# Rows of running decay sums through DRAM instead of through broadcast matmuls

## The chip, the cores and the metric

The kernel runs on one core of a Trainium2 chip. The metric is the device time of one execution in microseconds; the median over repeated executions stands for a kernel. Profiles come from one further execution that the hardware profiler records.

## The reference

Two layers of a decoder trunk work on 512 tokens of width 1024, all in float32. Each layer has a mixer and a gated feed-forward block with norms around both. The mixer projects the normed input into two groups: eight heads of dilated sliding-window attention, and four heads of a gated delta rule over chunks of 64 tokens. What the change touches is a part of the delta rule:

```python
g = jnp.cumsum(g, axis=-1)                       # within a chunk of 64 tokens
decay = jnp.exp(jnp.where(tril, g[..., :, None] - g[..., None, :], -jnp.inf))
kb = k * beta[..., None]
A = jnp.where(strict, jnp.einsum('bhnik,bhnjk->bhnij', kb, k) * decay, 0.0)
T = lax.linalg.triangular_solve(A + eye, eye, left_side=True, lower=True, unit_diagonal=True)
...
qk = jnp.einsum('bhnik,bhnjk->bhnij', q, k) * decay
```

For each head and each chunk a matrix of decays is needed: the exponential of the difference of two running sums, one that varies along the row and one along the column.

## The kernel before, in words

**Engines and helpers.** Every engine call goes through one helper (line 54), which gives the call a priority. So every row of a profile says L54, and the tiles' names tell where a row belongs. A scheduler then orders each engine's instructions by those priorities. Work that runs side by side is written as generators, which `nc.weave` interleaves: each has a number of steps and a stretch of the stage over which the steps are spread. Line numbers below are those of this kernel.

**The stage around the change.** In each layer, the channels of the delta rule's keys are projected first (`chan_proj` with `key`), woven with `decay()`, which makes the small vectors of the delta rule: `gr` holds the log decays, 128 tokens by 16 (four token blocks t times four heads h), and a matmul with the triangular matrix `tri` gives the running sums, whose negative is `ng`. Then five streams are woven: `dense` (32 steps: the q, k and v projections of the attention with four weight pieces each, four blocks of the delta rule's values, four of its queries, and the gate), `prepare` (16 steps over the first 0.43 of the stage), `attention` (from 0.52 to 0.9), `invert` (from 0.66 to 0.83) and `scan` (from 0.82 to 0.96).

**prepare().** After transposing the keys, it goes through the four token blocks. For each it makes the decay matrices `G` of the four heads: four matmuls broadcast a column of `gr` against `tri` into PSUM, VectorE adds `ng` (one value a partition) and the mask `dmask`, and ScalarE takes the exponential. Then PE multiplies the keys with themselves (`kT`), VectorE scales the product by `bb` and `G` into `U`, SP's queue stores `U` in the DRAM tile `dU`, and PE transposes `U` into `UT`. When all four `U` are stored, four loads, one a head, bring the diagonal 32 x 32 blocks back as `Lb` (64 KB each). GpSimd solves these blocks by forward substitution, 31 steps of a product (`Xt`) and a subtraction (`X`), and stores the result in `dX` by its own queue.

**invert().** For each token block GpSimd loads the solved blocks (`zc`) and clears `Z`, VectorE transposes the blocks into `Z`, and PE builds the whole inverse from them and `UT`; its first matmuls are `pw<-Z,UT`.

**Weights.** A weight piece (512 KB) is loaded by SP into one of three buffers `st`; ScalarE rounds it to `wh` (three buffers), VectorE, or for two pieces a layer GpSimd, takes the rest into `wl`, and PE uses both. The pieces of the attention are named `in_w_at`, those of the delta rule's channels `in_w_dn`. A buffer `st` is free for the next load when `wl` is done. SP carries all loads and stores named here in one order, except those of `dX` and `zc`.

**Buffers.** `G`, `UT`, `Kt`, `Z` and others share 41 buffers of one pool (`big`). The products in PSUM (`pw`) share four.

## Time and profile before

| | us |
|---|---|
| median of three runs | 1352.19 (1351.63 to 1352.3) |
| the profiled execution | 1352.82 |
| its span, first to last instruction | 1350.6 |
| PE busy | 1309.6 |
| VectorE busy | 1011.2 |
| ScalarE busy | 728.6 |
| GpSimd busy | 193.1 |

The profiled execution has 2.2 us outside its span. Its mean granted TensorE clock is 0.993 of full speed. A row of a timeline gives the start, the duration, the engine, the line, the operation with its output and inputs, the shape, how many instructions it stands for, and in brackets how long the engine had been idle and what ended that. PE is TensorE, DVE is VectorE, ACT is ScalarE, POOL is GpSimd; SPq and POOLq are the queues from which SyncE and GpSimd issue transfers.

### The profile page before, as it was taken

Reading aid. Unit: us, or ns where it says so; the run is one execution under the profiler, and the core shown is the slowest. Engines: PE = TensorE matmul, PEld = TensorE weight load, DVE = VectorE, ACT = ScalarE, POOL = GpSimd, SP = SyncE. Lnnn points to the kernel's source line nnn. Section 1 sums busy time; section 2 is a strip of 40 time slices with the busy share of each in tenths; the row PEclk is TensorE's granted clock in tenths of the full one; section 3 lists DMA queues with packets and bytes.
Section 4 is the critical chain, followed back from the end, with each engine's and each line's share of the span. In section 5 each row is a group of like instructions: output and inputs, shape, how many; then the busy total and the mean of one; then the engine's idle time right before and its main releaser. Section 6 shows DMA issues by size and latency. Waiting matters only on the chain.

```text
span 1350.6 us, 19526 instructions
## 1 busy us (share of the span) xinstructions
PE 1309.6 (97%) x6952; PEld 1090.6 (81%) x6952; DVE 1011.2 (75%) x1966; ACT 728.6 (54%) x1488; POOL 193.1 (14%) x250
## 2 busy tenths in 40 slices
PE   7999999999999999999999999998999999999997
PEld 6888877877988888887788877777888888888875
DVE  6565988868577787798777668888667767888885
ACT  5534976565333444467556369566543334444772
POOL 1007521011000000030010293102010000001201
PEclk8999999999999999999999999999999999999999
DMA  6233221244476566365651322104345666653664
GB/s 213 60 105 79 83 67 36 70 134 140 140 221 229 189 218 206 110 182 179 211 173 40 112 92 73 51 19 132 118 126 185 190 230 190 226 180 116 190 190 150
DMA packets 74274, 191.04 MB, mean 141 GB/s; under 512 B 13249, under 2 KB 13761, under 8 KB 74178
## 3 DMA queue, kind: packets, MB, share of 16 engines
q1 hardware_dynamic: 73666, 188.76, 44.4%
q0 software_dynamic: 512, 1.05, 0.4%
q8 instruction: 55, 0.90, 0.3%
q14 instruction: 41, 0.34, 0.1%
HBM read 159.89 MB, written 29.88 MB: 141 GB/s over the span
## 4 chain that ended last, share of the span: by engine, by line
PE 81%; DVE 8%; ACT 6%; DMA 2%; POOL 2%; issue 2%; SPq 0%; POOLq 0%; DVEq 0%; ACTq 0%
PE pm L54 68%; PE pw L54 12%; DVE wl L54 2%; ACT junk L54 2%; DVE xs L54 1%; ACT wh L54 1%; DMA st<-in_w_f 1%; POOL nr L54 1%; DVE x L54 1%; DVE xf L54 1%; ACT sc L54 1%; DMA stb<-in_w_ba 0%; POOL qs L54 0%; DVE KL L54 0%; POOL wl L54 0%
## 5 line engine op out<-in xcount | busy, mean ns | idle before, releaser
L54 DVE TENSOR_TENSOR wl<-st,wh 128x1024 fp32r<-128x1024 f32 (+1 forms) x246 | 280.9, 1146 | 164.7 <-ACT wh L54 163.6
L54 PE MATMUL pm<-hh,wh 128*128 128x512 f32 (+1 forms) x1024 | 374.4, 367 | 5.2 <-ACT hh L54 4.4
L54 PE MATMUL pm<-hl,wh 128*128 128x512 f32 (+1 forms) x1024 | 376.1, 368 | 2.2 <-DVE hl L54 2.2
L54 PE MATMUL pm<-hh,wl 128*128 128x512 f32 (+1 forms) x1024 | 374.9, 366 | 0.0
L54 ACT ACTIVATE wh<-st 128x1024 fp32r<-128x1024 f32 (+1 forms) x254 | 245.3, 971 | 239.2 <-PE pm L54 213.3
L54 PEld LDWEIGHTS pm<-hh,wh 128*128 128x128 f32 x1024 | 195.0, 191 | 35.5 <-ACT hh L54 4.8
L54 PEld LDWEIGHTS pm<-hl,wh 128*128 128x128 f32 x1024 | 195.9, 191 | 31.6 <-DVE hl L54 2.4
L54 PEld LDWEIGHTS pm<-hh,wl 128*128 128x128 f32 x1024 | 195.9, 191 | 29.3
L54 PE MATMUL pm<-wh,xf 128*128 128x512 f32 x528 | 164.5, 390 | 0.4 <-ACT wh L54 0.4
L54 PE MATMUL pm<-wh,hh 128*128 128x512 f32 x384 | 154.2, 404 | 0.0
L54 PE MATMUL pm<-wh,hl 128*128 128x512 f32 x384 | 152.7, 398 | 0.0
L54 PE MATMUL pm<-wl,hh 128*128 128x512 f32 x384 | 150.6, 394 | 0.8 <-DVE wl L54 0.8
L54 DVE SCALAR_TENSOR_TENSOR fgu<-pm,fw,fgu 128x511 f32<-128x511 f32 (+1 forms) x176 | 131.2, 746 | 23.1 <-ACT fgu L54 21.1
L54 PEld LDWEIGHTS pm<-wh,xf 128*128 128x128 f32 x528 | 99.0, 188 | 21.9 <-ACT wh L54 0.8
L54 PE MATMUL pm<-wl,xf 128*128 128x512 f32 x264 | 103.6, 392 | 0.8 <-DVE wl L54 0.8
L54 POOL TENSOR_TENSOR g<-g 128x256 f32<-128x256 f32 x22 | 25.4, 1173 | 494.2 <-DVE xf L54 494.2
L54 PEld LDWEIGHTS pm<-wl,hh 128*128 128x128 f32 x384 | 72.3, 188 | 15.0 <-DVE wl L54 1.8
L54 PEld LDWEIGHTS pm<-wh,hl 128*128 128x128 f32 x384 | 72.3, 188 | 14.1
L54 PEld LDWEIGHTS pm<-wh,hh 128*128 128x128 f32 x384 | 72.0, 188 | 14.2 <-ACT wh L54 0.5
L54 ACT ACTIVATE sc<-sc,mx 128x128 f32<-128x128 f32 (+3 forms) x128 | 69.5, 558 | 22.1 <-DVE mx L54 21.6
L54 ACT ACTIVATE fgu<-pm,fb,fw 128x512 f32<-128x512 f32 x88 | 66.9, 760 | 19.8 <-PE pm L54 19.8
L54 ACT ACTIVATE fgu<-fgu 128x512 f32<-128x512 f32 x44 | 27.8, 632 | 90.8 <-DVE fgu L54 90.8
(226 smaller groups left out, 1831.4 us busy)
## 6 DMA issues: line engine op xcount, KB each, us to landing
st<-in_w_f SPq DMA_DIRECT2D x118, 512.0 KB, 3.7
ws<-in_w_f SPq DMA_DIRECT2D x88, 256.0 KB, 4.6
T<-ws SPq DMA_DIRECT2D x66, 256.0 KB, 2.3
st<-in_w_at SPq DMA_DIRECT2D x32, 512.0 KB, 3.7
st<-T SPq DMA_DIRECT2D x30, 512.0 KB, 3.6
st<-in_w_dn SPq DMA_DIRECT2D x24, 512.0 KB, 3.7
st<-in_w_out SPq DMA_DIRECT2D x16, 512.0 KB, 3.7
U<-ws SPq DMA_DIRECT2D x22, 256.0 KB, 2.2
```

What stands on the lines that cost most here:

```text
L54: r = f(*args, **kwargs)
```

## The change

In each layer the 16 broadcast matmuls are gone. One matmul `gr`ᵀ · `tri` gives the same running sums with the 16 (block, head) pairs on partitions and the tokens along the row; VectorE copies them to `gt`, and SP stores them as `dG`, 16 x 128 values in DRAM. For each token block one load on SP then reads that block's four rows, 2 KB, to all 128 partitions of `G`. VectorE's additions work in place on `G` instead of reading PSUM. All else in `prepare` stands as it was.

```diff
         Gs, UT, Z = [], [], []
+
+        dG = dp.tile([NT * H, P], F32, name="dG")
 ...
             nc.scalar.activation(egl, pg[:, 16:], AF.Exp)
+
+            pgt = ps4(shape=(P, P))
+            nc.tensor.matmul(pgt[:16], gr, tri, start=True, stop=True)
+            gt = sp.tile([16, P], F32, name="gt", bufs=1)
+            nc.vector.tensor_copy(gt, pgt[:16])
+            nc.sync.dma_start(dG, gt)
             nc.vector.tensor_tensor(bd, pg[:, 16:], ng, op=OP.add)
 ...
             for t in range(NT):
-                pg2 = ps4()
+                G = big("G", shape=(P, H, P))
+                nc.sync.dma_start(G.rearrange("p h i -> p (h i)"), bcast(dG, H * P, t * H * P))
                 for h in range(H):
                     i = t * H + h
-                    nc.tensor.matmul(pg2[:, h, :], gr[:, i:i + 1].to_broadcast([P, P]), tri, start=True, stop=True)
-                G = big("G", shape=(P, H, P))
-                for h in range(H):
-                    i = t * H + h
-                    nc.vector.scalar_tensor_tensor(G[:, h, :], pg2[:, h, :], ng[:, i:i + 1], dmask,
+                    nc.vector.scalar_tensor_tensor(G[:, h, :], G[:, h, :], ng[:, i:i + 1], dmask,
                                                    op0=OP.add, op1=OP.add)
```

The scheduler orders the instructions anew. On SP, from the store of the first `U` to the last load of `Lb`, the first layer had this order before (the number behind a name is that of the buffer; the first `st` rows here are loads of v's pieces, the last is the first of `in_w_dn`):

```order
L54 DMA dU_588<-U_838 128x512
L54 DMA st_1234<-in_w_at 128x1024
L54 DMA st_1297<-in_w_at 128x1024
L54 DMA dU_588<-U_894 128x512
L54 DMA st_1340<-in_w_at 128x1024
L54 DMA dU_588<-U_966 128x512
L54 DMA dU_588<-U_995 128x512
L54 DMA Lb_823<-dU_588 16x32x32
L54 DMA st_1346<-in_w_at 128x1024
L54 DMA Lb_823<-dU_588 16x32x32 x3
```

With the change it has this one, from the store of the third `U` on; `st_1532` to `st_1864` are the first four pieces of `in_w_dn`:

```order
L54 DMA dU_594<-U_960 128x512
L54 DMA G_977<-dG_225 128x512
L54 DMA st_1532<-in_w_dn 128x1024
L54 DMA st_1657<-in_w_dn 128x1024
L54 DMA dU_594<-U_985 128x512
L54 DMA Lb_829<-dU_594 16x32x32 x2
L54 DMA st_1758<-in_w_dn 128x1024
L54 DMA Lb_829<-dU_594 16x32x32
L54 DMA st_1864<-in_w_dn 128x1024
L54 DMA Lb_829<-dU_594 16x32x32
```

The stores of `U` and the loads of `Lb` have moved back among the weight loads: the last `Lb` stood ahead of the first piece of `in_w_dn`, and now stands behind the fourth. Each of the second to fourth loads of `G` stands just behind the store of the `U` before it.

On VectorE, the rows around the fourth `U` before, where `wl_1067` belongs to k's last weight piece and `wl_1237` to v's first:

```order
L54 TENSOR_TENSOR wl_1067<-st_1064,wh_1066 128x1024
L54 SCALAR_TENSOR_TENSOR G_959<-pw_954,ng_217,dmask_88 128x128 x4
L54 SCALAR_TENSOR_TENSOR U_966<-pw_965,bb_215,G_959 128x128 x4
L54 SCALAR_TENSOR_TENSOR G_988<-pw_983,ng_217,dmask_88 128x128 x4
L54 SCALAR_TENSOR_TENSOR U_995<-pw_994,bb_215,G_988 128x128 x4
L54 TENSOR_TENSOR wl_1237<-st_1234,wh_1236 128x1024
```

And with the change, where `wl_1290` and `wl_1333` belong to v's second and third piece:

```order
L54 TENSOR_TENSOR r1_1154<-pm_920,rope_94 128x512
L54 TENSOR_TENSOR wl_1290<-st_1287,wh_1289 128x1024
L54 SCALAR_TENSOR_TENSOR G_977<-G_977,ng_217,dmask_88 128x128
L54 TENSOR_TENSOR wl_1333<-st_1330,wh_1332 128x1024
L54 SCALAR_TENSOR_TENSOR G_977<-G_977,ng_217,dmask_88 128x128 x3
L54 SCALAR_TENSOR_TENSOR U_985<-pw_984,bb_215,G_977 128x128 x4
L54 TENSOR_TENSOR r2_1155<-pm_920,rope_94 128x8x32 x2
```

The fourth `U` stood ahead of the split of v's first piece and now stands behind that of v's third.

On PE, the rows with the change around the first transpose of the first `U` (`U_840`); the keys' products for the second `U` (`kT`) are among them:

```order
L54 MATMUL pw_850<-ident_80,U_840 128x128
L54 MATMUL pw_857<-ident_80,r1_794 128x128
L54 MATMUL pw_850<-ident_80,U_840 128x128
L54 MATMUL pw_891<-kT_418 128x128
L54 MATMUL pw_850<-ident_80,U_840 128x128
L54 MATMUL pw_891<-kT_485 128x128
L54 MATMUL pw_850<-ident_80,U_840 128x128
L54 MATMUL pw_891<-kT_517 128x128
L54 MATMUL pw_891<-kT_586 128x128
L54 MATMUL pw_857<-ident_80,r1_794 128x128 x3
```

Behind them stand 20 matmuls of 128x512 for k, and then the first transpose of the second `U`. The broadcast matmuls that stood among such rows are gone; the matmuls of the dense work keep their order. On PE from the first `pw<-Z,UT` on, and on GpSimd throughout, the order is the one of before.

## The prediction

> **What bounds the kernel now.** I read the page's busy times first, then its chain of waits, then the group of the removed matmuls.

> ```profile
> PE 1309.6 (97%) x6952; PEld 1090.6 (81%) x6952; DVE 1011.2 (75%) x1966; ACT 728.6 (54%) x1488; POOL 193.1 (14%) x250
> PE 81%; DVE 8%; ACT 6%; DMA 2%; POOL 2%; issue 2%; SPq 0%; POOLq 0%; DVEq 0%; ACTq 0%
> ```

> TensorE is busy 97% of the span and carries 81% of the chain; GpSimd is busy 14%. So a matmul taken out counts, unless PE then meets something that was on time only because PE was no earlier. In each layer one such thing exists: the substitution X on GpSimd, whose result PE needs as `Z`. The timelines of GpSimd, VectorE and PE show how it ends (columns: start, us, engine, line, operation, count, idle time before it and what ended it):

> ```profile
> 105.72 0.23 POOL L54 TENSOR_TENSOR Xt<-Lb,X 64x31 f32<-64x31 f32 x1 [33.66 <-DMA Lb<-dU]
> 152.37 2.71 POOL L54 DMA_DIRECT2D dX<-X  x4 [0.31 <-POOL X L54]
> 166.88 2.40 POOL L54 TENSOR_TENSOR wl<-st,wh 128x1024 fp32r<-128x1024 f32 x1 [11.80 <-ACT wh L54]
> 174.55 0.59 POOL L54 DMA_DIRECT2D zc<-dX  x1 [5.26 <-DVE pTh L54]
> 175.15 2.42 POOL L54 TENSOR_TENSOR wl<-st,wh 128x1024 fp32r<-128x1024 f32 x1
> 177.51 0.53 POOL L54 MEMSET Z<- 128x512 f32 x1
> 178.07 0.30 DVE L54 STREAM_TRANSPOSE Z<-zc 32x128 f32<-32x128 f32 x1
> 179.48 0.41 PE L54 MATMUL pw<-Z,UT 32*32 32x32 f32 x8 [0.49 <-DVE Z L54]
> 842.56 0.41 PE L54 MATMUL pw<-Z,UT 32*32 32x32 f32 x8 [0.46 <-DVE Z L54]
> ```

> GpSimd begins when the last block of `dU` has come back as `Lb` (105.72), ends X at 152.37 - 0.31 = 152.06, and stores `dX`. It then loads `zc` at 174.55, and not for lack of `dX`: it waited for VectorE, which held the buffer. Behind that load stand a 2.4 us weight split and the memset of `Z`, then VectorE's transposes; PE gets to `Z,UT` 0.49 us (in the second layer 0.46 us) before they are done. So the chain already ends as PE comes, but X itself has slack. How much follows from the landing times, in the view of DMA issues (KB each, median us from issue to landing); the last row is that of the tile Lb:

> ```profile
> dU<-U SPq DMA_DIRECT2D x8, 256.0 KB, 2.0
> Lb<-dU SPq DMA_DIRECT2D x8, 64.0 KB, 4.2
> dX<-X POOLq DMA_DIRECT2D x8, 64.0 KB, 3.6
> zc<-dX POOLq DMA_DIRECT2D x8, 64.0 KB, 2.1
> st<-T SPq DMA_DIRECT2D x6, 256.0 KB, 3.2
> norm_post_mix<-in_norm_post_mix SPq DMA_DIRECT2D x4, 256.0 KB, 4.6
> DMA to landing us min/median/max: 2.2/4.2/5.4
> ```

> The fourth `dX` store is issued about 2.3 us after X ends and lands 3.6 us later, at 152.06 + 5.9 = 158.0. X could have ended 174.55 - 158.0 = 16.6 us later and delayed nothing.

> **The change, part by part. Matmuls: -3.35 us a layer while PE is fed.** The group view, three rows of PE's timeline, and the row of the tile G on VectorE (ns, first and last start):

> ```profile
> L54 PE MATMUL pw<-tri,gr 128*128 128x128 f32 x64 | 9.5, 275 | 0.0
> 56.15 0.40 PE L54 MATMUL pw<-gr,tri 128*128 128x16 f32 x2
> 69.47 1.05 PE L54 MATMUL pw<-tri,gr 128*128 128x128 f32 x8
> 70.37 1.06 PE L54 MATMUL pw<-kT 128*128 128x128 f32 x8
> L54 DVE SCALAR_TENSOR_TENSOR G<-pw,ng,dmask x16: 341/344/351, 71.6 to 92.3; 128x128 f32<-128x128 f32 x16
> ```

> Their idle time is 0.0: PE never waited for them. Eight of them push the next group back by 70.37 - 69.47 = 0.90 us, that is 0.1125 us each; 32 a layer make 3.6 us. The one matmul that is added is two such instructions, 0.22 us. PE would lead by about 3.35 us a layer, 6.7 us in all. The copy of `gt` on VectorE is 16 x 128, less than the 0.30 us that the 32 x 128 transpose above took, and lies just behind the row at 56.15; the store of `dG` (8 KB) lands like `dU` in about 2 us, more than ten microseconds before the first `G` is used at 71.6. On SP the first `G` load waits for that landing; behind it stand the loads of v's first two weight pieces, whose splits VectorE has in its order only behind the second and the third U. I cost these at nothing; uncovered, the copy and the landing would be 2.3 us once a layer.

> **The four loads of G: 0.5 us a layer.** Each moves 256 KB to 128 partitions. The trace has no such read from a freshly written DRAM row; the nearest rows are 3.2 us (`st<-T`, 256 KB out of DRAM scratch) and 4.6 us (`norm_post_mix`, a row broadcast to all partitions, the same shape of transfer), with 2.0 (`dU`) below. The second to fourth load stand on SP right behind the store of the `U` before, so they begin only when that `U` is done. VectorE and ScalarE then need this for the next one:

> ```profile
> 91.77 0.86 DVE L54 SCALAR_TENSOR_TENSOR G<-pw,ng,dmask 128x128 f32<-128x128 f32 x3
> 92.67 0.63 ACT L54 ACTIVATE G<-G 128x512 f32<-128x512 f32 x1 [0.79 <-DVE G L54]
> 93.33 1.13 DVE L54 SCALAR_TENSOR_TENSOR U<-pw,bb,G 128x128 f32<-128x128 f32 x4 [0.70 <-ACT G L54]
> ```

> That is 0.8 (the rest of U) + 0.33 (an issue) + 1.15 (four G) + 0.63 + 0.34 (the first U) = 3.25 us beside the landing, before PE can transpose the new `U`. By the order after, PE has 20 matmuls of 512 columns (0.23 us from one to the next) and 16 small ones like those above (0.11) between the first transpose of one `U` and that of the next, 6.4 us. So a landing of up to 3.1 us is hidden, 3.2 us stalls PE by 0.1, and 4.6 us by 1.5, once a layer, since more matmuls lie between the later ones. I take 0.5, nearer to `st<-T`, which too comes out of DRAM scratch; bounds 0 and 1.5. It leaves PE a lead of 2.85 us.

> **The wait that is moved: X begins 19 us later.** This is the term that decides. In the order after, the fourth `U` stands on VectorE behind the split of v's third weight piece, and on SP two of the four `Lb` loads stand behind loads of weight pieces. Before, all four were issued by 100.6:

> ```profile
> 96.65 0.33 SPq L54 DMA_DIRECT2D Lb<-dU  x1
> 98.71 0.33 SPq L54 DMA_DIRECT2D st<-in_w_at  x1
> 99.09 1.48 SPq L54 DMA_DIRECT2D Lb<-dU  x3
> 120.48 1.06 ACT L54 ACTIVATE wh<-st 128x1024 fp32r<-128x1024 f32 x1 [4.19 <-PE pm L54]
> 121.57 1.66 DVE L54 TENSOR_TENSOR wl<-st,wh 128x1024 fp32r<-128x1024 f32 x1 [4.68 <-ACT wh L54]
> ```

> The last `Lb` is now behind the load of the fourth piece of `in_w_dn`. There are three `st` buffers, so that load needs the buffer of the first piece, which VectorE frees with its `wl`: the row at 121.57, which waited for ScalarE, which waited for PE. With PE 2.85 us earlier, `wl` runs from 118.7 to 120.0 (its mean is 1.28 us, below), the weight load takes 0.33 to issue, and the last `Lb`, issued at 120.35, lands at 124.55 (122.5 with the least landing, 125.75 with the most). X starts 18.8 us later than at 105.72.

> How long X takes there depends on its neighbour. The same shape took 0.62 us in the second layer, and 2.69 us beside two weight splits on VectorE; the group rows count these splits from 105.7 to 152.1 and from 127.6 to 173.0, where X would lie by the work then beside it:

> ```profile
> 783.83 0.62 POOL L54 TENSOR_TENSOR Xt<-Lb,X 64x247 f32<-64x247 f32 x1
> 132.20 2.69 POOL L54 TENSOR_TENSOR Xt<-Lb,X 64x247 f32<-64x247 f32 x1
> 132.14 2.28 DVE L54 TENSOR_TENSOR wl<-st,wh 128x1024 fp32r<-128x1024 f32 x2
> L54 DVE TENSOR_TENSOR wl<-st,wh 128x1024 fp32r<-128x1024 f32 x8 | 10.1, 1277 | 8.1 <-ACT wh L54 8.1
> L54 DVE TENSOR_TENSOR wl<-st,wh 128x1024 fp32r<-128x1024 f32 x5 | 5.9, 1202 | 0.2 <-ACT wh L54 0.2
> ```

> A split costs X (2.69 - 0.62) / 2 = 1.0 us. X took 152.06 - 105.72 = 46.3 us; three splits fewer take 3 us off, and the busier VectorE of the later stretch (by its groups some seven more `v`, `Q` and `KL` operations of 512 columns, half as wide as a split and at about a third of its cost) gives, I estimate, two thirds of it back: 45.2 us, bounds 43.3 and 48. X ends at 169.75, the last `dX` lands 5.95 us later at 175.7. The split that was at 166.88 fits between X and that landing, and its weights are used only behind `Z,UT`. So `zc` is loaded at 175.7 instead of 174.55, and with the split, the memset and the transposes unchanged behind it PE starts `Z,UT` 1.15 us later than before, at 180.6. Without the wait it would be there at 179.48 - 0.49 - 2.85 = 176.1, so it stands idle 4.5 us. The whole lead of the layer is lost, and 1.15 us more. The spread is wide beside this: 2 us either way from `Lb`, 2 or 3 from X.

> **What the idle time does to the clock: +1.2 us a layer.** PE's timeline and two stretches of the windows (us, PE busy with its count, granted clock, DMA share, GB/s) show one such gap, and a row one that passed:

> ```profile
> 686.23 0.63 PE L54 MATMUL pw<-ident,xs 128*128 128x128 f32 x4 [2.12 <-DVE xs L54]
> 687.00:690.00 3.00, 3.00 (x16) 0.50 0.31 128
> 690.00:692.00 2.00, 2.00 (x17) 0.91 0.00 0
> 325.73 0.62 PE L54 MATMUL pm<-hh,wh 128*128 128x256 f32 x3 [2.09 <-ACT hh L54]
> ```

> Behind a gap of 2.12 us the granted clock was 0.50 for three microseconds and 0.91 in the next two, which costs 1.5 + 0.2 = 1.7 us of work; behind the gap of 2.09 us at 325.73 it stayed at 1.00. A gap of 4.5 us is twice as long, so I take 1.2 of the 1.7 (bounds 0 and 1.7). [...]

> **The sum.** Per layer +1.15 + 1.2 = +2.35 (the -3.35 and the +0.5 are inside the 1.15, since the wait ends on its own time); two layers alike in order and rows give +4.7. Against the profiled execution, 1352.82 us (span 1350.6 and 2.2 around it), that is 1357.5; it stands 0.63 above the median of 1352.19, so the forecast is 1356.9.

> **Rivals.**
> 1. *The lead survives.* X ends early enough for PE's lead: this needs 4 us a layer off the chain, for instance the least landing of `Lb` (-2.0) and X at 43.3 us (-1.9). It decides from a `dX` landing at 171.7 or sooner. Then two leads of about 3 us remain, -6.0: 1346.2. For it: the spread of just those rows. Against it: both must come out at their ends, in both layers.
> 2. *It comes out even.* Half of that, or the chain as computed with the clock left alone: +2.3 and less, 1352 to 1354.5. For it: the gap at 325.73, and every small gain in X.
> 3. *Slower still.* G lands like the broadcast rows (4.6 us: PE, and with it the split that frees the last `Lb`, 1.0 us later), X takes its old 46.3 us, and the clock costs 1.5: 2 x (1.15 + 1.0 + 1.1 + 1.5) = +9.5, 1361.7. For it: the transfer has the shape of the broadcast, and the second stretch has VectorE busier.

> That the change does nothing is no rival: the order after has the one matmul and not the 16.

> **Chances.** Forecast (1355 to 1360) 0.35, the first rival 0.17, the second 0.31, the third 0.17. A difference under 0.2% (2.7 us) can hardly be told from none in a measurement of this kernel; so faster has the first rival's 0.17, same the second's 0.31, slower 0.52. The range goes from the upper half of the first rival's cases to the third's sum: 1348 to 1363.

> **What would show it.** Right: PE waits 4 to 5 us at `pw<-Z,UT` for VectorE's Z in both layers, GpSimd's idle time before `zc` ends with `dX` and not with VectorE, X starts near 124, the fourth `Lb` is issued near 120 behind a weight load, and the clock falls below 1 just behind both waits. The matmul term is wrong if PE's first v block is not about 3 us early. The forecast fails if `zc` still waits for VectorE, or if PE stalls longer at `ident,U` than at `Z,UT`.

## The result

| | before | after |
|---|---|---|
| median, us | 1352.19 (1351.63 to 1353.99) | 1365.49 (1363.52 to 1366.85) |
| profiled execution, us | 1352.82 | 1365.49 |
| its span | 1350.6 | 1362.8 |
| mean granted clock | 0.993 | 0.987 |

The change makes the kernel slower by 1%: the ratio is 1.0099, with a 95% interval of 1.0086 to 1.0112. The forecast was slower, by 4.7 us; measured are 13.3, and 1365.49 lies above the range's end of 1363.

**Where the time is.** The page's busy times and chain of waits after, and two rows of PE's waits (us in total, times, longest):

```profile
PE 1309.6 (96%) x6892; PEld 1088.1 (80%) x6892; DVE 1011.2 (74%) x1968; ACT 729.8 (54%) x1488; POOL 193.1 (14%) x250
PE 75%; DVE 7%; ACT 5%; POOL 5%; DMA 4%; issue 2%; SPq 0%; POOLq 0%; DVEq 0%; ACTq 0%
```

```profile
PE pw L54 <- DVE Z L54: 9.9, 6, 4.7
PE pw L54 <- DVE U L54: 2.7, 3, 1.3
```

PE has 60 recorded instructions fewer (6892 against 6952) and is busy exactly as long as before, 1309.6 us; what the matmuls gave, slower matmuls took (mean granted clock 0.987 against 0.993). The span grew by 12.2 us of idle PE, and GpSimd and DMA, at 2% each of the chain before, now carry 5% and 4%. PE's waits for Z rose to 9.9 us (before: 1.6), those for U are new.

A second reading puts the drift to places. It takes the start of the first matmul of a kind in each layer in both timelines, and subtracts:

| stretch of PE's work | layer 1 | layer 2 | forecast |
|---|---|---|---|
| first `gr,tri` to first `K,Q` (the prepare part) | -1.07 | -1.43 | -2.85 |
| to the first `Z,UT` | +4.15 | +4.61 | +4.0 |
| to the first `R,Z` (the inverse and the scan's start) | +2.32 | +3.32 | +1.2 |

Ahead of the first layer's row, between the layers and behind the second lie -0.73, +1.26 and -0.23 us, together +0.30; the whole is 12.2 us. The forecast for the second row is the lead of 2.85 given back and 1.15 more.

**The wait at Z.** GpSimd, VectorE and PE in the timeline after:

```profile
125.26 0.23 POOL L54 TENSOR_TENSOR Xt<-Lb,X 64x31 f32<-64x31 f32 x1 [53.54 <-DMA Lb<-dU]
171.62 2.70 POOL L54 DMA_DIRECT2D dX<-X  x4 [0.31 <-POOL X L54]
174.33 2.42 POOL L54 TENSOR_TENSOR wl<-st,wh 128x1024 fp32r<-128x1024 f32 x1
176.97 0.58 POOL L54 DMA_DIRECT2D zc<-dX  x1 [0.22 <-ACT Q L54]
180.42 0.30 DVE L54 STREAM_TRANSPOSE Z<-zc 32x128 f32<-32x128 f32 x1 [4.08 <-POOL Z L54]
181.83 0.60 PE L54 MATMUL pw<-Z,UT 32*32 32x32 f32 x8 [4.47 <-DVE Z L54]
851.67 0.60 PE L54 MATMUL pw<-Z,UT 32*32 32x32 f32 x8 [4.73 <-DVE Z L54]
```

X starts at 125.26 instead of 105.72, GpSimd works almost without a pause from there to the load of `zc` at 176.97, and PE stands idle 4.47 and 4.73 us at `Z,UT`. Why X starts late is on SP's queue:

```profile
109.76 0.33 SPq L54 DMA_DIRECT2D dU<-U  x1
112.29 0.87 SPq L54 DMA_DIRECT2D Lb<-dU  x2
116.98 0.35 SPq L54 DMA_DIRECT2D st<-in_w_dn  x1
117.38 0.43 SPq L54 DMA_DIRECT2D Lb<-dU  x1
121.10 0.35 SPq L54 DMA_DIRECT2D st<-in_w_dn  x1
121.49 0.43 SPq L54 DMA_DIRECT2D Lb<-dU  x1
```

The data of all four `Lb` were in DRAM when the first two loads went out at 112.29. The fourth went out 9.2 us later, each of the last two right behind a weight load that had waited for its buffer (SP stood 6.9 us in these two waits, both for VectorE's `wl`). Before, none of these pieces stood ahead of an `Lb`: the last `st` row in the listing of SP's order before is v's fourth piece, as its name `in_w_at` says, and the first of the `in_w_dn` pieces was loaded at 109.78.

**The clock behind it.** The windows (us, busy time of each engine, granted clock, DMA share, GB/s) of the stretches that the clock was low, and of the one behind the first:

```profile
180.50:187.30 6.80, 5.47 (x27) 3.73 (x28) 5.25 (x12) 2.25 (x3) 0.52 (x3) 0.50 0.21 78
849.50:859.70 10.20, 8.03 (x56) 6.04 (x56) 6.27 (x13) 2.96 (x5) 1.44 (x4) 0.50 0.30 91
187.40:190.00 2.60, 2.60 (x35) 2.25 (x35) 1.82 (x6) 0.62 (x2) 0.35 (x1) 1.00 0.49 170
```

The clock drops to 0.50 while PE still waits and stays there for 6.8 us in the first layer and 10.2 in the second. Of these PE worked 5.5 and 8.0 us at half speed. Apart from these two stretches and the end of the run, the clock was low for 13.7 us in the profile after, as in the one before.

**The loads of G.** The windows of PE alone over the prepare part, before and after, then VectorE and PE in the timeline after, then the DMA issues after:

```profile
56.15:133.57 77.42, 77.42 (x408) 1.00 0.30 86
```

```profile
55.42:131.77 76.35, 74.89 (x377) 1.00 0.33 101
87.26 1.14 DVE L54 SCALAR_TENSOR_TENSOR G<-G,ng,dmask 128x128 f32<-128x128 f32 x4 [3.44 <-DMA G<-dG]
89.50 0.33 PE L54 MATMUL pw<-ident,U 128*128 128x128 f32 x1 [1.03 <-DVE U L54]
99.91 0.33 PE L54 MATMUL pw<-ident,U 128*128 128x128 f32 x1 [0.41 <-DVE U L54]
G<-dG SPq DMA_DIRECT2D x8, 256.0 KB, 4.0
Lb<-dU SPq DMA_DIRECT2D x8, 64.0 KB, 3.2
dX<-X POOLq DMA_DIRECT2D x8, 64.0 KB, 2.7
```

A load of G took 4.0 us (3.5 to 4.7). VectorE stood 3.44 us for the second one, and PE 1.03 us for the second U and 0.41 for the third. PE was idle 76.35 - 74.89 = 1.46 us in a part where it had not been idle at all.

### The profile page after: what moved, and what is told of

Read it like the earlier page. It is cut to its first block, busy times and chain, and to the rows that moved or that the text cites. A ratio compares the mean times of both kernels' runs of the same rounds, so it can differ in the third digit from the quotient of the medians.

```text
span 1362.8 us, 19456 instructions
## 1 busy us (share of the span) xinstructions
PE 1309.6 (96%) x6892; PEld 1088.1 (80%) x6892; DVE 1011.2 (74%) x1968; ACT 729.8 (54%) x1488; POOL 193.1 (14%) x250
## 3 DMA queue, kind: packets, MB, share of 16 engines
q1 hardware_dynamic: 74882, 190.87, 43.3%
q0 software_dynamic: 512, 1.05, 0.4%
## 4 chain that ended last, share of the span: by engine, by line
PE 75%; DVE 7%; ACT 5%; POOL 5%; DMA 4%; issue 2%; SPq 0%; POOLq 0%; DVEq 0%; ACTq 0%
PE pm L54 64%; PE pw L54 12%; DVE wl L54 2%; POOL X L54 2%; ACT junk L54 2%; POOL Xt L54 1%; ACT wh L54 1%; DMA G<-dG 1%; DVE xs L54 1%; DVE x L54 1%; POOL nr L54 1%; DVE r L54 1%; DVE xf L54 1%; DMA st<-in_w_f 1%; DMA stb<-in_w_ba 0%
## 5 line engine op out<-in xcount | busy, mean ns | idle before, releaser
L54 DVE TENSOR_TENSOR wl<-st,wh 128x1024 fp32r<-128x1024 f32 (+1 forms) x246 | 280.6, 1144 | 154.0 <-ACT wh L54 149.7
L54 PE MATMUL pm<-hh,wh 128*128 128x512 f32 (+1 forms) x1024 | 375.4, 368 | 5.3 <-ACT hh L54 4.3
L54 PE MATMUL pm<-hl,wh 128*128 128x512 f32 (+1 forms) x1024 | 377.2, 369 | 2.4 <-DVE hl L54 2.4
L54 PE MATMUL pm<-hh,wl 128*128 128x512 f32 (+1 forms) x1024 | 376.1, 368 | 0.0
L54 ACT ACTIVATE wh<-st 128x1024 fp32r<-128x1024 f32 (+1 forms) x254 | 245.6, 972 | 232.7 <-PE pm L54 204.8
L54 PEld LDWEIGHTS pm<-hh,wh 128*128 128x128 f32 x1024 | 195.7, 192 | 35.8 <-ACT hh L54 4.8
L54 PEld LDWEIGHTS pm<-hl,wh 128*128 128x128 f32 x1024 | 196.4, 192 | 31.5 <-DVE hl L54 2.6
L54 PEld LDWEIGHTS pm<-hh,wl 128*128 128x128 f32 x1024 | 196.3, 192 | 29.3
L54 PE MATMUL pm<-wh,xf 128*128 128x512 f32 x528 | 164.6, 391 | 0.0
L54 PE MATMUL pm<-wh,hh 128*128 128x512 f32 x384 | 153.0, 401 | 0.0
L54 PE MATMUL pm<-wh,hl 128*128 128x512 f32 x384 | 152.8, 399 | 0.0
L54 PE MATMUL pm<-wl,hh 128*128 128x512 f32 x384 | 150.7, 394 | 0.8 <-DVE wl L54 0.8
L54 DVE SCALAR_TENSOR_TENSOR fgu<-pm,fw,fgu 128x511 f32<-128x511 f32 (+1 forms) x176 | 131.1, 745 | 23.1 <-ACT fgu L54 21.1
L54 PEld LDWEIGHTS pm<-wh,xf 128*128 128x128 f32 x528 | 99.2, 188 | 21.2 <-ACT e L54 0.6
L54 PE MATMUL pm<-wl,xf 128*128 128x512 f32 x264 | 103.6, 393 | 0.4 <-DVE wl L54 0.4
L54 POOL TENSOR_TENSOR g<-g 128x256 f32<-128x256 f32 x22 | 25.4, 1172 | 494.2 <-DVE xf L54 493.9
L54 ACT ACTIVATE sc<-sc,mx 128x128 f32<-128x128 f32 (+3 forms) x128 | 69.5, 557 | 31.0 <-DVE mx L54 30.5
L54 PEld LDWEIGHTS pm<-wl,hh 128*128 128x128 f32 x384 | 72.3, 188 | 15.1 <-DVE wl L54 2.0
L54 PEld LDWEIGHTS pm<-wh,hh 128*128 128x128 f32 x384 | 72.1, 189 | 14.6 <-ACT wh L54 0.5
L54 PEld LDWEIGHTS pm<-wh,hl 128*128 128x128 f32 x384 | 72.4, 188 | 13.9
L54 ACT ACTIVATE fgu<-pm,fb,fw 128x512 f32<-128x512 f32 x88 | 66.9, 761 | 19.8 <-PE pm L54 19.8
L54 ACT ACTIVATE fgu<-fgu 128x512 f32<-128x512 f32 x44 | 27.8, 632 | 90.8 <-DVE fgu L54 90.7
## 6 DMA issues: line engine op xcount, KB each, us to landing
ws<-in_w_f SPq DMA_DIRECT2D x88, 256.0 KB, 4.7
T<-ws SPq DMA_DIRECT2D x66, 256.0 KB, 2.1
U<-ws SPq DMA_DIRECT2D x22, 256.0 KB, 2.1
```

Source lines behind the costliest of these rows:

```text
L54: r = f(*args, **kwargs)
```

## The experiments

The theory at this point: the price is the late start of X, paid at Z and again in the clock; the loads of G only eat a part of the gain. The rival: the broadcasts through DRAM are the price, and the wait at Z comes on top of time that is lost anyway. The first two runs each undo one of the two in the changed kernel.

**Only the loads of Lb on another queue.**

```diff
-                nc.sync.dma_start(Lb[h * 16:h * 16 + 16], src)
+                nc.gpsimd.dma_start(Lb[h * 16:h * 16 + 16], src)
```

> The changed kernel with one edit: the four loads of Lb in each layer are issued by GpSimd's queue instead of SP's, so they no longer stand behind the loads of in_w_dn. Order on PE and VectorE is that of the changed kernel. Theory (the late start of X, through the wait at Z and the clock behind it, is what the change costs): the fourth U is stored at 109.8 us as in the changed kernel, X starts near 117 instead of 125.3 and ends near 164, zc waits for VectorE again, PE does not wait at the first Z,UT, the clock stays at 1.00 behind it. Each layer then keeps the lead of about 1.1 us that PE still had at its first K,Q: 1352.2 - 2 = about 1350. Rival (the loads of G and their stalls are what costs, the wait at Z comes on top of lost time): 1358 or more, with the wait at Z gone.

Measured: 1351.43 us against 1352.92 of the kernel before on the same chip, a ratio of 0.9988 (0.9976 to 1.0). The timeline of GpSimd and PE of this run:

```profile
112.47 2.71 POOL L54 DMA_DIRECT2D Lb<-dU  x4 [40.33 <-DMA dU<-U]
117.69 0.23 POOL L54 TENSOR_TENSOR Xt<-Lb,X 64x31 f32<-64x31 f32 x1 [2.51 <-DMA Lb<-dU]
163.28 2.52 POOL L54 DMA_DIRECT2D dX<-X  x4 [0.29 <-POOL X L54]
173.33 0.59 POOL L54 DMA_DIRECT2D zc<-dX  x1 [5.10 <-DVE pTh L54]
178.25 0.41 PE L54 MATMUL pw<-Z,UT 32*32 32x32 f32 x8 [0.50 <-DVE Z L54]
```

X starts at 117.69 and `zc` waits for VectorE again, as before the change; PE's wait at Z is back at 0.50 us, and the clock stays at 1.00 from the prepare part to the scan in both layers. This one edit, which moves eight transfers of 64 KB to another queue, takes back the change's whole loss: 14.1 us between the medians. The rival, 1358 or more, falls. What is left is 1.5 us between the medians, which the interval can hardly tell from none; in the profile, PE's way from `gr,tri` to the first `R,Z` is 0.9 and 1.1 us shorter than before. The matmuls alone would give 6.7 in all.

**Only the loads of G, all ahead of the loop.**

```diff
+            Gl = []
+            for t in range(NT):
+                Gl.append(big("G", shape=(P, H, P)))
+                nc.sync.dma_start(Gl[t].rearrange("p h i -> p (h i)"), bcast(dG, H * P, t * H * P))
             for t in range(NT):
-                G = big("G", shape=(P, H, P))
-                nc.sync.dma_start(G.rearrange("p h i -> p (h i)"), bcast(dG, H * P, t * H * P))
+                G = Gl[t]
```

> The changed kernel with one edit: the four loads of G in each layer are issued one behind the other ahead of the loop over the token blocks, instead of each in its turn. On SP the stores of U and the loads of Lb come back to where they stood before the change. Theory: no load of G is waited for (all land before 85 us), X starts near 103 in the first layer, no wait at Z,UT beyond half a microsecond, and the whole lead of 3.35 us a layer is kept: 1352.2 - 6.7 = about 1345.5. Rival (256 KB broadcasts cost in any place, by their traffic or their landing of 4.0 us): PE waits at ident,U for DMA, and the time stays at 1350 or above.

Measured: 1345.95 us against 1352.92, a ratio of 0.9956 (0.9941 to 0.997): the fastest kernel of this study, faster than both. Its windows of PE over the prepare part, rows of its timeline, and its loads of G:

```profile
54.91:129.32 74.41, 74.41 (x377) 1.00 0.35 103
101.13 0.23 POOL L54 TENSOR_TENSOR Xt<-Lb,X 64x31 f32<-64x31 f32 x1 [29.91 <-DMA Lb<-dU]
170.06 0.58 POOL L54 DMA_DIRECT2D zc<-dX  x1 [5.25 <-DVE pTh L54]
174.99 0.41 PE L54 MATMUL pw<-Z,UT 32*32 32x32 f32 x8 [0.52 <-DVE Z L54]
G<-dG SPq DMA_DIRECT2D x8, 256.0 KB, 5.8
```

PE is never idle in the prepare part, which is 77.42 - 74.41 = 3.01 us shorter than before (2.97 in the second layer). Four loads at once land later, 5.8 us, and nobody notices, since they are issued 7.3 us and more ahead of use. From `gr,tri` to the first `R,Z` PE gains 3.3 us in each layer, and the medians differ by 7.0 us, close to the 6.7 that the matmuls were priced at. The run with `Lb` moved is 5.5 us slower; that is about what the loads of G in their turn still cost. The broadcast through DRAM is thus not dear in itself; its place is. Issued in its turn, each load puts its landing between one U and the next, and it pushes the last U, its store and the loads of Lb back among the weight loads.

**X late, and nothing else.** These runs take the kernel before the change and put products without use on GpSimd between the landing of Lb and the substitution; the order on all engines is otherwise that of before. First with 27 of them:

```diff
+            for _ in range(27):
+                tmp = xp.tile([64, 256], F32, name="Xt", tag="Xt")
+                nc.gpsimd.tensor_tensor(tmp.rearrange("p (n m) -> p n m", n=16), Lb[:, 0, 16:]..., X[:, 0, None, 0:16]..., op=OP.mult)
             for j in range(NB - 1):
```

> The kernel before the change, with 27 more GpSimd products (64x256, from Lb and X into the scratch tile Xt, results unused) in each layer between the landing of Lb and the substitution, some 0.7 us each beside VectorE's work: X ends about 19 us later, as in the changed kernel, and nothing else is changed. Theory: zc is loaded near 177, PE waits about 2.8 us at the first Z,UT of each layer, +2.35 us a layer, and the granted clock falls behind it: +4.7 without and up to +11 with the clock, 1357 to 1363. Rival (X's start is not what costs): within 2 us of before.

Measured: 1369.21 us against 1352.92, a ratio of 1.0128 (1.0108 to 1.0148), 16.3 us slower and outside what was expected. Timeline and windows of this run:

```profile
105.03 23.37 POOL L54 TENSOR_TENSOR Xt<-Lb,X 64x256 f32<-64x256 f32 x28 [33.01 <-DMA Lb<-dU]
174.14 2.71 POOL L54 DMA_DIRECT2D dX<-X  x4 [0.31 <-POOL X L54]
184.68 0.60 PE L54 MATMUL pw<-Z,UT 32*32 32x32 f32 x8 [5.25 <-DVE Z L54]
857.73 0.60 PE L54 MATMUL pw<-Z,UT 32*32 32x32 f32 x8 [5.88 <-DVE Z L54]
181.90:192.10 10.20, 7.42 (x42) 5.45 (x44) 6.27 (x13) 2.75 (x5) 2.02 (x5) 0.50 0.31 84
```

The products took 0.83 us each, not 0.7; X ended 2.5 us later than in the changed kernel, and PE waited 5.25 and 5.88 us. The clock was at 0.50 for 10.2 us behind each wait. So the late X alone, without any of the change, can cost as much as the change and more.

With 14 products:

> As the run with 27 more products, with 14: X ends about 10 us later. Theory: the slack of 16.6 us covers it, the time is that of before within 1.5 us, and zc still waits for VectorE. If X's lateness costs in proportion instead, half of what 27 products cost, some 3 to 5 us.

Measured: 1352.21 us, a ratio of 0.9998 (0.9987 to 1.0009).

```profile
103.91 13.35 POOL L54 TENSOR_TENSOR Xt<-Lb,X 64x256 f32<-64x256 f32 x15 [32.98 <-DMA Lb<-dU]
162.77 2.71 POOL L54 DMA_DIRECT2D dX<-X  x4 [0.31 <-POOL X L54]
173.31 0.58 POOL L54 DMA_DIRECT2D zc<-dX  x1 [5.24 <-DVE pTh L54]
```

X ends 10.4 us later than before (13.7 in the second layer) and the time does not move: X has slack, at least that much of the 16.6 us that the prediction read from the landing of `dX`, and the cost is not in proportion to the lateness. Nor do 13 us of products beside VectorE's work cost anything by themselves. Between 14 and 27 lies the edge:

> As the runs with 27 and 14 more GpSimd products, with 22; in the run with 27 one product took 0.83 us (23.37 us for 28) and PE waited 5.25 us at the first Z,UT. Five fewer: X ends some 4.2 us earlier, PE waits about 1.1 us there instead of 0.49, +0.6 us a layer, and no clock loss, since no idle time that short has lowered the clock in the runs so far: 1352.9 + 1.2 = about 1354. If the clock falls behind any idle time here, 1357 or more.

Measured: 1356.83 us against 1352.82 on that chip, a ratio of 1.003 (1.0018 to 1.0041): 4.0 us slower, not 1.2. The clock stayed at 1.00 in both layers, but the wait was not at Z. Timeline of GpSimd, VectorE and PE:

```profile
171.87 2.39 POOL L54 TENSOR_TENSOR wl<-st,wh 128x1024 fp32r<-128x1024 f32 x1
171.78 3.04 DVE L54 SCALAR_TENSOR_TENSOR v<-v,acc 128x512 f32<-128x512 f32 x1
175.27 0.51 PE L54 MATMUL pw<-pT,va 128*128 128x256 f32 x2 [2.03 <-DVE pT L54]
```

GpSimd's weight split, which the late X had pushed back, ran beside VectorE's `v<-v,acc`. That took 3.04 us; the same operation took 0.69 us in the kernel before. VectorE was late for `pT`, and PE waited 2.03 us there, and 0.69 us at the same place in the second layer; together that is 2.7 of the 3.0 us by which this profile's span exceeds that of before. So a late X can cost at a second place, before the chain at Z is reached; the expectation had left that out. That the split held VectorE's operation up is a reading of these two rows, and no run took them apart; GpSimd's split itself took 2.39 us, as before (2.40).

> As the run with 27 more products, with 24: three fewer, X ends some 2.5 us earlier and PE waits about 2.7 us at the first Z,UT, +2.2 us a layer by the wait alone: 1357.5 with the clock at 1.00 in both layers. If the loss in clock goes with the length of the idle time, some 2 us a layer more, 1361. If it comes in whole steps as in the runs so far (1.7, 3.4 or 5.1 us of clock lost), 1361 to 1365 where both layers are hit.

Measured: 1363.31 us against 1352.82, a ratio of 1.0092 (1.007 to 1.0114), 10.5 us slower. PE's waits and the windows around the low clock:

```profile
180.76 0.60 PE L54 MATMUL pw<-Z,UT 32*32 32x32 f32 x8 [2.88 <-DVE Z L54]
851.06 0.41 PE L54 MATMUL pw<-Z,UT 32*32 32x32 f32 x8 [3.60 <-DVE Z L54]
179.50:186.75 7.25, 5.99 (x30) 4.25 (x31) 5.70 (x13) 2.58 (x4) 0.90 (x3) 0.53 0.25 72
852.00:855.50 3.50, 3.50 (x18) 2.25 (x15) 2.81 (x6) 1.83 (x3) 0.00 (x0) 0.55 0.05 20
```

The waits are near the 2.7 us expected, and the time is well above the 1357.5 of the waits alone. The low clock lasted 6.8 us behind the wait of 2.88 us and 3.4 us behind the longer one of 3.60. That speaks against a loss that goes with the length of the wait, and for whole steps. Two products more than in the run with 22 cost 6.5 us between the medians. Of the 6.2 us between the two profiles' spans, 4.0 lie behind the waits at Z, where the clock was low. X ended 1.2 us earlier in this run than in the changed kernel, in both layers, so this is the closest match to its lateness.

## Why the prediction was wrong in size

**The place, the order of events and the sign were right.** The last Lb was issued behind the load of the fourth piece of `in_w_dn` at 121.49 (forecast 120.35), X started at 125.26 (124.55) and took 171.31 - 125.26 = 46.05 us (45.2), `zc` was loaded at 176.97 (175.7), PE waited 4.47 us at Z (4.5), and the clock fell behind that. That the wait came out at 4.5 is partly luck: PE arrived 1.3 us later than forecast (177.36 for 176.1), and `Z` was ready 1.2 us later (181.83 for 180.6). The sign that GpSimd's idle time before `zc` ends with `dX` did not show: GpSimd ran the weight split from 174.33 to 176.75 and loaded `zc` 0.22 us later, so the profile does not tell whether the split or the landing of `dX` came last. The run with Lb on its own queue shows that this chain carries the whole loss; the runs with a late X show the same in the kernel before. Of the slack of 16.6 us, the run with 14 products bears out 10.4 (13.7 in the second layer); in the run with 22, where X ended 16.8 us later, the time had already moved, by another way than the one at Z.

**The matmul term was right, and hidden at first.** The run with G loaded ahead gives 3.01 and 2.97 us a layer by the first `K,Q`, and 3.3 by the first `R,Z`, for the 3.35 forecast.

**"The four loads of G: 0.5 us a layer" failed.** Of the 3.0 us that PE could lead by, 1.07 and 1.43 were left at the first `K,Q`, so the loads cost 1.9 and 1.5 us, at or above the bound of 1.5. The landing was 4.0 us, nearer to the broadcast rows (4.6) than to `st<-T` (3.2) on which the step had settled. By the step's own room of 3.1 us a landing of 4.0 stalls PE by 0.9; 1.03 was seen at the second U. The step's "once a layer" did not hold in the first layer, where the third U stalled PE by 0.41 as well; in the second layer only the second U did, by 1.29. Some 0.5 us more are in busy time (74.89 against 74.41 with G ahead), and what makes them was not tried. The chain at Z runs on PE's progress until the last Lb: that load waits for a `wl` of VectorE, which stood 2.89 us for ScalarE (at 119.85), and ScalarE waits for PE: 4.19 us at this place in the profile before, 2.39 us after, where the profile shows no releaser. So the lost lead was not hidden in the wait at Z.

**"X begins 19 us later" was nearly right.** The drift from `K,Q` to `Z,UT` was +4.15 and +4.61 where +4.0 was forecast. The last Lb was issued 1.1 us later than forecast, in part because PE had lost more of its lead; X took 0.85 us more, and the landing of Lb was shorter than the 4.2 taken (125.26 - 121.49 = 3.8).

**"What the idle time does to the clock: +1.2 us a layer" failed.** It measured +2.32 and +3.32. The step took one low stretch of the profile before, 3.4 us and 1.7 us lost, as the most that could come, and discounted it. After the change the clock was low for 6.8 and 10.2 us. Here the bound itself was wrong, and the profile before could have shown it: near its start stands a low stretch of 6.8 us, which began within an idle time of 2.24 us (windows of PE, before):

```profile
17.93:24.76 6.83, 5.67 (x26) 0.50 0.71 192
```

The +2.32 and +3.32 are themselves those of one execution: over the five executions of the changed kernel the mean granted clock goes from 0.984 to 0.988, and the span is longest where the clock is lowest.

Summed against the forecast of +4.7: the lead +3.2 (1.78 and 1.42), the chain +0.8, the clock +3.2 (1.12 and 2.12), and +0.3 outside the stretches of the table, 7.5 in all, which makes 12.2 of span. The prediction calls the range's end of 1363 the third rival's sum; that sum is 1361.7.

**The rivals.** "The lead survives" did not happen in the change, and did in the run with G ahead. "It comes out even" did not happen either; the run with Lb on its own queue comes near it. "Slower still" had the right ingredients, G landing like a broadcast and X of the old length, and still priced the clock at 1.5.

## What to carry to other kernels

When a transfer takes the place of engine work, price the order that it forces on the queue before its own duration: what stands behind a load that waits for a buffer waits too (here the fourth `Lb`, which went out 9.2 us after the first two). Issue such loads together and well ahead of use, where even a longer landing hides (5.8 us against 4.0, issued 7.3 us and more ahead), and not each in its turn. And price new idle time of PE twice, for the wait and for the clock behind it. In these profiles the second price came in whole steps of 3.4 us at half speed, none to three of them for waits of two to six microseconds, and the length of the wait alone did not give their number.

## What the hardware showed that was not expected

The length of an idle time does not decide whether the clock falls. Rows of PE and windows of the run with 14 products, then of the run with 24:

```profile
686.47 0.63 PE L54 MATMUL pw<-ident,xs 128*128 128x128 f32 x4 [2.78 <-DVE xs L54]
683.50:694.00 10.50, 7.72 (x66) 1.00 0.55 190
```

```profile
998.60 0.62 PE L54 MATMUL pm<-hh,wh 128*128 128x256 f32 x3 [1.90 <-ACT hh L54]
999.12:1002.53 3.41, 2.83 (x14) 0.50 0.79 290
```

An idle time of 2.78 us left the clock at 1.00; one of 1.90 us lowered it. What goes with the fall in these traces is how much of the idle time lies in one step of the grid. Windows of PE in the profile before, cut at the grid, around its idle times of 2.09 us (up to 325.73) and 2.12 us (up to 686.23):

```profile
321.72:325.13 3.41, 1.92 (x13) 1.00 0.27 71
325.13:328.54 3.41, 2.21 (x16) 1.00 0.85 259
683.53:686.94 3.41, 1.29 (x12) 1.00 0.83 253
```

Of the 2.09 us, 1.49 lay in one step and 0.60 in the next, and the clock stayed at 1.00; the 2.12 us lay in one, and the clock fell to 0.50 at its end. In the traces before and after together, each of the 11 steps at full clock in which PE was idle for 1.94 us or more was followed by a low one; in nine of them PE worked for 0.29 to 1.47 us. Of the other 760, with 1.69 us of idle time or less, none was. That is the count of these two profiles alone. The 1.90 us of the run with 24 lay within one step too, which ended at 999.12.

The number of low steps goes with how long PE was idle in the first of them. In the traces before and after, and in the stretches read of the runs with 24 and 27, that was 0.58 us or less in the nine stretches of one step, 0.84 to 1.35 in the three of two steps, and 2.18 to 3.35 in the three of three. This fits the wait of 2.88 us that cost two steps and that of 3.60 that cost only one: PE resumed 0.84 us after the clock had fallen in the first case, and 1.29 us before in the second. All this is read from these traces alone; no run placed an idle time on the grid on purpose, and none of these stretches lies between 1.35 and 2.18 us. It was not tried whether work on PE during the wait would keep the clock up.
